# A two-layer hybrid encoder on eight cores: feature-major activations, layer norms by ones-matmuls, two tiles half a layer apart, packed weights

## The chip, the cores and the metric

The kernel runs on all eight cores of one Trainium2 chip (two dies of four cores). The metric is the device time of one execution on the slowest core, in microseconds (us). The times of this kernel come in two states. In the fast state all eight cores show the same granted TensorE clock; in the slow state one die or both show a lower one and the run is some per cent longer.

Names in the text and the profiles: PE is TensorE (matmuls), DVE VectorE, ACT ScalarE, POOL GpSimd, SP SyncE, which here only issues transfers. HBM is the chip's memory, SBUF a core's own, PSUM where TensorE puts its results. A transfer lands when its last data have arrived; its landing time counts from its issue.

## The reference

Each core takes one stream of 8192 rows of 1024 features (16 tiles of 512 rows) and one sample tile of 256 rows. Each of two layers does this:

```python
proj = x @ w_in                                   # 1024 -> 2048
u, v, xb, gb, gc, h = split(proj)                 # 512, 512, 256, 256, 256, 256
out_a = u * spatial_gate(layer_norm(v))           # 128-row chunks, 8 heads
out_b = pool_mixer(xb)                            # trailing means 2/4/8/16, minus xb, then 64x64 maps
out_c = gb * conv3(gc * h)
x = layer_norm(ALPHA * x + concat(out_a, out_b, out_c) @ w_out)
x = layer_norm(ALPHA * x + (silu(x @ w_gate) * (x @ w_up)) @ w_down)   # inner width 2816
# ... states of pool and conv, the normalised v of the sample rows
```

Weights and activations arrive as fp32; both kernels multiply in bf16. One tile of 512 rows through one layer is called a *tile-layer* below. A core does 32 of them, plus two of half the size.

## The kernel before

Weights are converted once per run from fp32 to bf16 in HBM, by casting DMAs on POOL's software queue. For every tile-layer they are streamed again, in 47 units of up to 512 KB, into a ring of 15 slots in SBUF, on SP's hardware queue. A ring load waits for the conversion of its unit and for its slot.

```python
def emit_conv(l, ui):                        # on POOL's queue; reads pieces of 1 to 4 KB, writes 512 B to 2 KB
    ...
    if k[0] == "in":
        src = w_in[l, kc0*128:(kc0+nk)*128, c0:c0+512].rearrange("(k p) n -> p k n", p=128)
        jobs.append((dst.rearrange("p (k n) -> p k n", k=nk), src, 0))
    ...

def emit_load(n):                            # on SP's queue
    ti, l, ui = seq[n]
    s_ = n % NSLOT
    S.add("sp", lambda e: e.dma_start(out=ring[:, s_, 0:ne], in_=wbf[l, ui][:, 0:ne]), ...)
```

The residual lies row-major (`xres`, rows on partitions). After each norm it is cast to `xbf` and transposed on TensorE into `xT`, which the next product reads:

```python
def transpose_chunk(c):
    b = alloc1()
    for k in range(8):
        S.add("pe", lambda e, k=k: e.transpose(out=psb(b)[:, k, :], in_=xbf[:, c, k*128:(k+1)*128], identity=idb[:]), ...)
    S.add("act", lambda e: e.copy(out=xT[:, :, c*128:(c+1)*128], in_=psb(b)), ...)
```

The output and down projections (`tm_proj_ln`, matmuls at L765) keep the activations stationary, so that rows come out on partitions; the norm is then 1024 wide, on DVE and ACT:

```python
def stage_a(c):   # DVE: xres = ALPHA*xres + psum, with row sum; ACT: Square with row sum
    S.add("dve", lambda e: e.scalar_tensor_tensor(out=xres[:, c, :], in0=xres[:, c, :], scalar=ALPHA, in1=..., accum_out=lsum[:, c:c+1]), ...)
    ...
def stage_b(c):   # DVE: reciprocal, last pass; ACT: xbf = bf16(xres)
    ...
# one tile after the other, both layers
for ti in range(len(tiles)):
    for l in range(2):
        tile_layer(ti, l, (ti * 2 + l) * NUNIT)
```

Of the kernel before, what the change touches and what calls it, by code (L numbers as in the profile page):

```python
# [12 lines left out]
DFF = 2816  # L13
NFC = 22
ALPHA = float(4 ** 0.25)
EPS = 1e-5
NSLOT = 15
NUNIT = 47
U_V0, U_V1, U_XB, U_GC, U_H, U_U01, U_U23, U_GB, U_OUT0, U_GU0, U_DN0 = 0, 1, 2, 3, 4, 5, 6, 7, 8, 12, 36
N_CORES = 8  # L20
NPT_FULL = 16

# [155 lines left out]

def build(npt, with_sample=True):
    nc = bass.Bass("TRN2", target_bir_lowering=False)  # L180
    NP = npt * 512
# [7 lines left out]
    xp = din("xp", [NP, D])  # L189
    xs = din("xs", [256, D])  # L190
    spool = din("spool", [2, 60, 256])
    sconv = din("sconv", [2, 8, 256])
    ln_mix_g = din("ln_mix_g", [2, D]); ln_mix_b = din("ln_mix_b", [2, D])
    ln_ffn_g = din("ln_ffn_g", [2, D]); ln_ffn_b = din("ln_ffn_b", [2, D])
    v_norm_g = din("v_norm_g", [2, 512]); v_norm_b = din("v_norm_b", [2, 512])
    w_in = din("w_in", [2, D, 2048])
    w_spatial = din("w_spatial", [2, 8, 128, 128])
    b_spatial = din("b_spatial", [2, 8, 128])
    w_pool = din("w_pool", [2, 4, 64, 64])
    pool_scale = din("pool_scale", [2, 256])  # L200
    conv_w = din("conv_w", [2, 3, 256])
    w_out = din("w_out", [2, D, D])
    w_gate = din("w_gate", [2, D, DFF]); w_up = din("w_up", [2, D, DFF])
    w_down = din("w_down", [2, DFF, D])
    ident = din("ident", [128, 128])
    cst = din("cst", [128, 34])

    yp = dout("yp", [NP, D])
    ys = dout("ys", [256, D])
    o_pool_p = dout("o_pool_p", [2, 15, 256])  # L210
    o_pool_s = dout("o_pool_s", [2, 60, 256])
    o_conv_p = dout("o_conv_p", [2, 2, 256])
    o_conv_s = dout("o_conv_s", [2, 8, 256])
    o_v = dout("o_v", [2, 256, 512])

    wbf = nc.dram_tensor("wbf", [2, NUNIT, 128, 2048], BF16).ap()
# [3 lines left out]
    xres = sb("xres", [128, 4, D], F32)  # L220
    xbf = sb("xbf", [128, 4, D], BF16)
    xT = sb("xT", [128, 8, 512], BF16)
    vscr = sb("vscr", [128, 2, 512], F32)
# [6 lines left out]
    cat = sb("cat", [128, 8, 512], BF16)  # L230
    hid = sb("hid", [128, NFC, 512], BF16)
    sscr = sb("sscr", [128, 2, 512], F32)
    lscr = sb("lscr", [128, 2, D], F32)
    mixg = sb("mixg", [128, D], F32); mixb = sb("mixb", [128, D], F32)
    ffng = sb("ffng", [128, D], F32); ffnb = sb("ffnb", [128, D], F32)
    vng = sb("vng", [128, 512], F32); vnb = sb("vnb", [128, 512], F32)
# [3 lines left out]
    ctmp = sb("ctmp", [128, 2, 512], F32)  # L240
    idf = sb("idf", [128, 128], F32)
    idb = sb("idb", [128, 128], BF16)
    cst_sb = sb("cst_sb", [128, 34], F32)
    pscale = sb("pscale", [128, 2, 2], F32)
    cw = sb("cw", [128, 2, 2, 3], F32)
# [3 lines left out]
    stin = sb("stin", [64, 256], F32)  # L249
    stin2 = sb("stin2", [8, 256], F32)  # L250
    sttm = sb("sttm", [128, 1, 256], F32)
    sttm2 = sb("sttm2", [128, 1, 256], F32)
    vst = sb("vst", [128, 4, 6], F32); vmv = sb("vmv", [128, 4, 2], F32); vrs = sb("vrs", [128, 4], F32)
    lsum = sb("lsum", [128, 4], F32); lmean = sb("lmean", [128, 4], F32)
    lnb = sb("lnb", [128, 4], F32); lsq = sb("lsq", [128, 4], F32); lrs = sb("lrs", [128, 4], F32)
# [3 lines left out]
    st = {"pb": 0, "cv": 0, "ld": 0, "io": 0}  # L259
# [6 lines left out]
    def alloc2():  # L266
        if st["pb"] % 2:
            st["pb"] += 1
        b = st["pb"] % 8
        st["pb"] += 2  # L270
        return b

# [3 lines left out]
    def psb(b):  # L276
        return ps[:, b, :].bitcast(BF16).rearrange("p (k n) -> p k n", k=8)

    UL = [("in", 512, 0, 4), ("in", 512, 4, 4)]
    for c0 in (1024, 1536, 1792, 0, 256, 1280):  # L280
        UL.append(("inF", c0))
    for j in range(4):
        UL.append(("out", j))
    for g in range(6):
        for j in range(4):
            UL.append(("gu", g, j))
    for j in range(11):
        UL.append(("down", j))
    assert len(UL) == NUNIT

    def unit_keys(l, ui):
        if UL[ui][0] == "gu":
            return [("wbf", l, ui, 0), ("wbf", l, ui, 1)]
        return [("wbf", l, ui, 0)]

    def emit_conv(l, ui):
        k = UL[ui]
        dst = wbf[l, ui]
        jobs = []
        if k[0] == "in":  # L300
            _, c0, kc0, nk = k
            src = w_in[l, kc0 * 128:(kc0 + nk) * 128, c0:c0 + 512].rearrange("(k p) n -> p k n", p=128)
            jobs.append((dst.rearrange("p (k n) -> p k n", k=nk), src, 0))
        elif k[0] == "inF":
            c0 = k[1]
            src = w_in[l, :, c0:c0 + 256].rearrange("(k p) n -> p k n", p=128)
            jobs.append((dst.rearrange("p (k n) -> p k n", k=8), src, 0))
        elif k[0] == "out":
            j = k[1]
            src = w_out[l, j * 256:(j + 1) * 256, :].rearrange("(k p) n -> p k n", p=128)  # L310
            jobs.append((dst.rearrange("p (k n) -> p k n", k=2), src, 0))
        elif k[0] == "gu":
            _, g, j = k
            nf = 4 if g < 5 else 2
            f0 = 4 * g
            for wi, wsrc in enumerate((w_gate, w_up)):
                src = wsrc[l, j * 256:(j + 1) * 256, f0 * 128:(f0 + nf) * 128].rearrange("(k p) n -> p k n", p=128)
                d = dst[:, wi * 2 * nf * 128:(wi + 1) * 2 * nf * 128].rearrange("p (k n) -> p k n", k=2)
                jobs.append((d, src, wi))
        else:  # L320
            j = k[1]
            src = w_down[l, j * 256:(j + 1) * 256, :].rearrange("(k p) n -> p k n", p=128)
            jobs.append((dst.rearrange("p (k n) -> p k n", k=2), src, 0))
        for d, s_, wi in jobs:
            ch = st["cv"] % 8
            st["cv"] += 1
            S.add("pool", lambda e, d=d, s_=s_: e.dma_start(out=d, in_=s_),
                  writes=[("wbf", l, ui, wi), ("cvch", ch)], dma_chan=("cv", ch))

    tiles = [("p", t) for t in range(npt)] + ([("s", 0)] if with_sample else [])  # L330
    seq = [(ti, l, ui) for ti in range(len(tiles)) for l in range(2) for ui in range(NUNIT)]

    def emit_load(n):
        ti, l, ui = seq[n]
        s_ = n % NSLOT
        ne = 1024 if (UL[ui][0] == "gu" and UL[ui][1] == 5) else 2048
        S.add("sp", lambda e: e.dma_start(out=ring[:, s_, 0:ne], in_=wbf[l, ui][:, 0:ne]),
              reads=unit_keys(l, ui), writes=[("ring", s_)], dma_chan=("w", s_))

    def slot(n):  # L340
        assert n < st["ld"], (n, st["ld"])
        return n % NSLOT

    def done(n):
        m = n + NSLOT
        assert m == st["ld"], (m, st["ld"])
        if m < len(seq):
            emit_load(m)
        st["ld"] += 1

    def tile_src(ti):
        kind, t = tiles[ti]
        if kind == "p":
            return xp[t * 512:(t + 1) * 512, :], yp[t * 512:(t + 1) * 512, :], 4
        return xs, ys, 2

    def load_xres(ti):
        src, _, nch = tile_src(ti)
        for c in range(nch):
            S.add("pool", lambda e, c=c: e.dma_start(out=xres[:, c, :], in_=src[c * 128:(c + 1) * 128, :]),  # L360
                  writes=[("xres", c)], dma_chan=("xl", c))

    def load_xbf(ti):
        src, _, nch = tile_src(ti)
        for c in range(nch):
            S.add("pool", lambda e, c=c: e.dma_start(out=xbf[:, c, :], in_=src[c * 128:(c + 1) * 128, :]),
                  writes=[("xbf", c)], dma_chan=("xb", c))

    load_xbf(0)
    load_xres(0)  # L370
    for l in range(2):
        for ui in range(NUNIT):
            emit_conv(l, ui)
    for n in range(5):
        emit_load(n)

    def pdma(fn, reads=(), writes=()):
        ch = st["io"]
        st["io"] += 1
        return S.add("sp", fn, reads=list(reads), writes=list(writes), dma_chan=("pr", ch))  # L380

    pdma(lambda e: e.dma_start(out=idf[:], in_=ident), writes=["idf"])
    pdma(lambda e: e.dma_start(out=cst_sb[:], in_=cst), writes=["cst"])
    S.add("act", lambda e: e.copy(out=idb[:], in_=idf[:]), reads=["idf"], writes=["idb"])
    S.add("dve", lambda e: e.memset(epst[:], EPS), writes=["eps"])
# [20 lines left out]
    for var, src_bf, keys in ((0, catA, [("cat", j) for j in range(4)]), (1, catB, [("cat", j) for j in range(4, 8)])):  # L406
        for l in range(2):
# [7 lines left out]
            if var == 0:  # L415
                S.add("dve", lambda e, s0=s0: e.memset(wsT[64:128, s0:s0 + 8, 0:64], 0.0), writes=[("wsT", s0)])
# [495 lines left out]
```

## Time and profile before

| | before |
|---|---|
| three first runs | 6115.57, 6364.31, 6601.76 us (median 6364.31) |
| fast runs (all batches) | 6107 to 6139 us |
| one tile-layer in mid-run, clock 0.99 to 1.00 | 170.2 us |

The page of the profile of the kernel before: first each engine's busy time, its share of the span and its number of instructions; then the span in 40 slices of about 157 us, in tenths (PE busy, PE's granted clock, DMA engines busy); then the shares of the chain of waits that ended last.

```profile
PE 5665.5 (90%) x29197; PEld 2825.2 (45%) x29684; DVE 2400.3 (38%) x4131; ACT 1674.3 (27%) x2801; POOL 532.4 (8%) x622
...
PE   0865799999999999999999999999999999999987
...
PEclk9977899999999999999999999999999888888877
DMA  9999645454455545454544445554555434443354
...
PE 73%; DVE 11%; DMA 10%; ACT 2%; issue 2%; POOL 1%; another core or an unknown queue 1%; DVEq 0%; POOLq 0%; SPq 0%; ACTq 0%
```

TensorE is the bound from within the fifth slice on. Before that the DMA engines are full and PE is not. This profiled execution was one of the slower ones: the clock falls in the last quarter. A tile-layer at 0.81 takes 200.1 us instead of 170.2.

The timeline of PE in mid-run, kernel before. The columns are: start, duration, engine, line, operation, out<-in, shape, count, and in brackets the idle time just before and what ended it. The last line starts the same stage one tile-layer later, and so gives the 170.2 us.

```profile
3129.49 0.39 PE L707 MATMUL ps<-diff,wpbd 128*128 128x512 bf16 x1 [0.40 <-DVE cat L699]
...
3133.63 13.98 PE L765 MATMUL ps<-ring,cat 128*128 128x512 bf16 x62
3147.44 1.06 PE L464 MATMUL ps<-idb,xbf 128*128 128x128 bf16 x16
3150.16 7.15 PE L814 MATMUL ps<-xT,ring 128*128 128x256 bf16 x64 [1.66 <-ACT xT L466]
3158.09 1.15 PE L464 MATMUL ps<-idb,xbf 128*128 128x128 bf16 x16 [0.78 <-ACT sscr L817]
3161.18 69.32 PE L814 MATMUL ps<-xT,ring 128*128 128x256 bf16 x346 [1.94 <-ACT xT L466]
...
3303.83 13.98 PE L765 MATMUL ps<-ring,cat 128*128 128x512 bf16 x63
```

Each pair of transposed chunks (L464) costs 1.1 us of PE and then 1.7 to 1.9 us of waiting for ACT to copy the result out of PSUM.

The waits of PE from 710 us to the end, kernel before (engine, tile and line, releaser: total us, times, longest):

```profile
PE ps L814 <- ACT xT L466: 107.9, 62, 1.9
...
PE ps L707 <- DVE sscr L694: 36.0, 29, 6.6
```

The start costs as much as two tile-layers: PE runs without gaps from 713 us on, and until then it has done two tile-layers, 340 us of work. So 373 us are lost there.

### The profile page before, as it was taken

The numbers are of one execution on the slowest core, as the hardware profiler recorded it, in microseconds if no ns is written. First come the engines' busy times: TensorE is split into PE (matmuls) and PEld (weight loads), VectorE is DVE, ScalarE is ACT, GpSimd is POOL, SyncE is SP. The second block draws the span as 40 slices with busy tenths as digits, with TensorE's granted clock in tenths as the row PEclk, the third lists the DMA queues.
The fourth block names the chain that finished last, engine by engine and source line by source line (L and its number), as shares of the span: only waits on it lengthen the run. The fifth ranks groups of instructions, "written<-read, shape, count | busy, mean of one in ns | idle before, by whom it ended". The sixth has DMA issues, their size and how long they took to land.

```text
span 6285.8 us, 71667 instructions; the slowest of 8 cores (6193.5 to 6285.8 us)
## 1 busy us (share of the span) xinstructions
PE 5665.5 (90%) x29197; PEld 2825.2 (45%) x29684; DVE 2400.3 (38%) x4131; ACT 1674.3 (27%) x2801; POOL 532.4 (8%) x622
## 2 busy tenths in 40 slices
PE   0865799999999999999999999999999999999987
PEld 0422344444444444444444444444444444444454
DVE  0331344333344444444333444444444323442322
ACT  0221232222223232322232322323232222222212
POOL 2111000000000000000000000000000000000000
PEclk9977899999999999999999999999999888888877
DMA  9999645454455545454544445554555434443354
GB/s 134 183 162 161 197 160 184 156 172 163 145 188 174 171 158 185 165 181 165 181 161 160 168 152 190 166 176 161 183 166 181 144 116 170 135 169 128 120 192 155
DMA packets 347184, 1033.95 MB, mean 164 GB/s; under 512 B 42036, under 2 KB 82406, under 8 KB 346854
## 3 DMA queue, kind: packets, MB, share of 16 engines
q1 hardware_dynamic: 268550, 894.39, 42.0%
q0 software_dynamic: 78304, 134.94, 11.4%
q8 instruction: 234, 3.83, 0.3%
q14 instruction: 96, 0.79, 0.0%
HBM read 1057.85 MB, written 83.01 MB: 181 GB/s over the span
## 4 chain that ended last, share of the span: by engine, by line
PE 73%; DVE 11%; DMA 10%; ACT 2%; issue 2%; POOL 1%; another core or an unknown queue 1%; DVEq 0%; POOLq 0%; SPq 0%; ACTq 0%
PE ps L814 37%; PE ps L765 24%; PE ps L575 8%; DMA wbf<-w_gate 3%; DMA wbf<-w_up 3%; PE ps L515 3%; DVE xres L749 2%; DVE xres L727 2%; DVE lscr L740 2%; DMA wbf<-w_in 1%; DVE diff L660 1%; ACT xT L466 1%; PE ps L464 1%; DMA wbf<-w_down 1%; DMA xbf<-xp 1%
## 5 line engine op out<-in xcount | busy, mean ns | idle before, releaser
L814 PE MATMUL ps<-xT,ring 128*128 128x512 bf16 (+1 forms) x13824 | 2667.8, 357 | 188.0 <-ACT xT L466 114.4
L814 PEld LDWEIGHTS ps<-xT,ring 128*128 128x128 bf16 x14016 | 1419.2, 102 | 1422.2 <-issue 308.9
L765 PE MATMUL ps<-ring,hid 128*128 128x512 bf16 x5676 | 1323.6, 393 | 57.2 <-DMA ring<-wbf 49.1
L819 DVE TENSOR_TENSOR hid<-sscr,ps 128x512 bf16<-128x512 f32 (+1 forms) x876 | 517.2, 596 | 2211.6 <-PE ps L814 2116.0
L817 ACT ACTIVATE sscr<-ps 128x512 f32<-128x512 f32 (+1 forms) x876 | 454.2, 524 | 2063.8 <-PE ps L814 2054.3
L765 PEld LDWEIGHTS ps<-ring,hid 128*128 128x128 bf16 x5808 | 581.0, 101 | 777.4 <-issue 196.4
L575 PE MATMUL ps<-xT,ring 128*128 128x512 bf16 (+1 forms) x3182 | 746.9, 387 | 16.0 <-DVE sscr L694 8.6
L727 DVE SCALAR_TENSOR_TENSOR xres<-xres,ps 128x1024 f32<-128x1024 f32 x264 | 321.9, 1219 | 1095.7 <-PE ps L765 1095.7
L731 ACT ACTIVATE xbf<-xres 128x1024 bf16<-128x1024 f32 x264 | 279.0, 1057 | 1387.3 <-DVE xres L727 1387.1
L575 PEld LDWEIGHTS ps<-xT,ring 128*128 128x128 bf16 x3264 | 315.4, 101 | 382.2 <-issue 91.9
L765 PE MATMUL ps<-ring,cat 128*128 128x512 bf16 x2064 | 476.5, 390 | 3.5 <-DMA ring<-wbf 0.6
L765 PEld LDWEIGHTS ps<-ring,cat 128*128 128x128 bf16 x2112 | 210.8, 100 | 263.6 <-issue 58.6
L515 PE MATMUL ps<-ring,xT 128*128 128x512 bf16 x1023 | 247.2, 394 | 65.3 <-ACT xT L466 63.3
L466 ACT COPY xT<-ps 128x1024 bf16<-128x1024 bf16 x264 | 254.7, 1017 | 142.8 <-PE ps L464 142.8
L645 POOL TENSOR_TENSOR pscr<-xbuf 128x526 f32<-128x526 f32 (+1 forms) x64 | 71.3, 1113 | 2345.9 <-ACT xbuf L582 2172.9
L753 ACT CAST xbf<-xres 128x1024 bf16<-128x1024 f32 x198 | 206.9, 1045 | 226.5 <-DVE xres L749 226.5
L464 PE MATMUL ps<-idb,xbf 128*128 128x128 bf16 x2112 | 151.1, 226 | 85.5 <-DMA xbf<-xp 51.6
L755 POOL DMA_DIRECT2D yp<-xres x64 | 34.2, 535 | 1893.4 <-DVE xres L749 1873.5
L515 PEld LDWEIGHTS ps<-ring,xT 128*128 128x128 bf16 x1056 | 104.8, 101 | 195.7 <-issue 76.7
L464 PEld LDWEIGHTS ps<-idb,xbf 128*128 128x128 bf16 x2112 | 133.1, 101 | 125.4 <-DMA xbf<-xp 52.8
L678 POOL TENSOR_TENSOR ybuf<-ybuf,ctmp 128x512 f32<-128x512 f32 (+1 forms) x128 | 180.5, 1420 | 5.0
L749 DVE SCALAR_TENSOR_TENSOR xres<-lscr,lrs,ffnb 128x1024 f32<-128x1024 f32 x132 | 169.6, 1285 | 7.7 <-DVE lrs L748 0.5
(94 smaller groups left out, 2447.5 us busy)
## 6 DMA issues: line engine op xcount, KB each, us to landing
ring<-wbf SPq DMA_DIRECT2D x1462, 512.0 KB, 6.1
ring<-wbf SPq DMA_DIRECT2D x136, 256.0 KB, 4.5
xres<-xp POOLq DMA_DIRECT2D x64, 512.0 KB, 12.7
yp<-xres POOLq DMA_DIRECT2D x64, 512.0 KB, 6.4
mixg<-ln_mix_g SPq DMA_DIRECT2D x34, 512.0 KB, 5.7
mixb<-ln_mix_b SPq DMA_DIRECT2D x34, 512.0 KB, 4.8
ffng<-ln_ffn_g SPq DMA_DIRECT2D x34, 512.0 KB, 11.5
ffnb<-ln_ffn_b SPq DMA_DIRECT2D x34, 512.0 KB, 12.0
```

Source lines behind the costliest of these rows:

```text
L464: S.add("pe", lambda e, k=k: e.transpose(out=psb(b)[:, k, :], in_=xbf[:, c, k * 128:(k + 1) * 128], identity=idb[:]), reads=[("xbf", c), " ...
L466: S.add("act", lambda e: e.copy(out=xT[:, :, c * 128:(c + 1) * 128], in_=psb(b)), reads=[PS(b)], writes=[("xT", c)])
L515: S.add("pe", lambda e, c=c, kc=kc, b=b, w=w: e.matmul(ps[:, b, :], lhsT=xT[:, kc, c * 128:(c + 1) * 128], rhs=w, start=(kc == 0), stop=(k ...
L575: S.add("pe", lambda e, kc=kc, b=b, w=w: e.matmul(ps[:, b, 0:T], lhsT=w[:, kc, j * 128:(j + 1) * 128], rhs=xT[:, kc, 0:T], start=(kc == 0) ...
L727: S.add("dve", lambda e: e.scalar_tensor_tensor(out=xres[:, c, :], in0=xres[:, c, :], scalar=ALPHA, in1=ps[:, pb:pb + 2, :].rearrange("p a ...
L731: S.add("act", lambda e: e.activation(out=xbf[:, c, :], in_=xres[:, c, :], func=AF.Square, accum_out=lsq[:, c:c + 1]), reads=[XK], writes= ...
L749: S.add("dve", lambda e: e.scalar_tensor_tensor(out=xres[:, c, :], in0=lscr[:, c % 2, :], scalar=lrs[:, c:c + 1], in1=bet[:], op0=ALU.mult ...
L753: S.add("act", lambda e: e.copy(out=xbf[:, c, :], in_=xres[:, c, :]), reads=[XK], writes=[("xbf", c)])
L765: S.add("pe", lambda e, k=k, hf=hf, w=w: e.matmul(ps[:, pb + hf, :], lhsT=src[:, k, c * 128:(c + 1) * 128], rhs=w[:, hf * 512:(hf + 1) * 5 ...
L814: S.add("pe", lambda e, kc=kc, b=b, w=w: e.matmul(ps[:, b, t0:t1], lhsT=w[:, kc % 2, fi * 128:(fi + 1) * 128], rhs=xT[:, kc, t0:t1], start ...
L817: S.add("act", lambda e: e.activation(out=sscr[:, f % 2, t0:t1], in_=ps[:, banks[0], t0:t1], func=AF.Silu), reads=[PS(banks[0])], writes=[ ...
L819: S.add("dve", lambda e: e.tensor_tensor(out=hid[:, f, t0:t1], in0=sscr[:, f % 2, t0:t1], in1=ps[:, banks[1], t0:t1], op=ALU.mult), reads= ...
```

## The change

The intent: take the transposes and their copies away by keeping the features on partitions all through; compute the norm's sums over features with matmuls against ones; hide the norm of one tile behind the products of another; and store the weights packed, so that each conversion reads whole 8 KB rows. Cut to its core:

```diff
-UL = [("in", 512, 0, 4), ...]      # 47 units; pieces of 512 B to 2 KB written
+wpk = din("wpk", [2, NUNIT, 128, 2048])          # 45 units, packed on the host
+wbf = nc.dram_tensor("wbf", [2, NUNIT, 128, WROW], BF16).ap()      # WROW = 2304
+    S.add("pool", lambda e: e.dma_start(out=wbf[l, ui, :, 0:2048], in_=wpk[l, ui]), ...)
-NSLOT = 15
+NSLOT = 10
-def transpose_chunk(c): ...                       # 64 PE transposes and 8 ACT copies per tile-layer
-def tm_proj_ln(...): ...                          # row-major products and 1024-wide norms
+def acc(tl, which, l, d, b):                      # feature block d of 8; beside the product
+    S.add("dve", ... xr = xr*ALPHA*g + psum ...)                   # L487
+    S.add("act", ... Square(xr + bias) ...)                        # L490
+    S.add("dve", ... S1 += xr + bias ...)                          # L495
+    S.add("dve", ... S2 += square ...)                             # L497
+def ln_task(tl, which, l):                        # in small steps, in the background
+    # S1, S2 split into bf16 high and low (L510, L511), four ones-matmuls (L519),
+    # mean, variance, Sqrt, 512-wide reciprocal (L530), then per block:
+    S.add("dve", ... xr = xr + bias - mu ...)                      # L538
+    S.add("dve", ... xr = xr * rsd ...)                            # L540
+    S.add("act", ... xt = xr*g + b, bf16 ...)                      # L547
-for ti in range(len(tiles)):
-    for l in range(2): tile_layer(ti, l, ...)
+# stage_order: in/out of tile A, second half of gate/up and down of tile B,
+# first half of gate/up of A, in/out of B, second half and down of A, first half of B, ...
+for o in order:
+    for pe_us, dve_us in stage(o):
+        bg.advance(max(0.1 * pe_us, 0.9 * pe_us - dve_us))         # norm steps by credit
 # head pairs of the spatial gate
+        if j == 1:                                 # the pooling matmuls: after pair 1, were after pair 3
+            ... ps = wpbd * diff ...                               # L743
```

Two more moves: the order converts layer 0 first and needs layer 1 only after two and a half tiles, where before the first tile needed both, one after the other. And the sample tile runs early, among the prompt tiles, where before it ran last. Besides, the host now hands over the inputs with features first and turns the outputs back (`make_in_maps`, `gather`), so the transposes of the first layer's input are gone from the chip altogether; host time is not in the metric.

## The prediction

> **What bounds it now.** TensorE: in the stretch table it is busy 153 of every 160 us from 800 us on; the chain of waits is 73% PE, 11% DVE, 10% DMA. One tile-layer (512 rows, one layer) in mid-run takes 170.2 us on the PE timeline at granted clock 0.99. Its 730 matmuls of 512 columns run at 216 ns (gate/up: 69.2 us for 320), so 157.7 us is the product itself. The other 12.5 us: 64 transposes (4.2 us) and waits for the transposed copy and the pooling result (about 8 us).
>
> Two other costs. Start: until 670 us the DMA engines are full (0.97 to 1.05) while weights are converted to bf16; at 710 us one tile (340 us of work) is done, so about 370 us are lost. Clock: on core 2 it is 0.81 from 4900 us on, on core 0 until 1600 us; a tile-layer then takes 200.1 us. The Trainium skill, "TensorE: Matmul & The Clock Gate", Part 1, names such a 13/16 limit; the 0.81 agrees, though all cores also run long at 0.99. Unthrottled, before would take about 6060 us; the spread 6115 to 6602 is, I think, time at 0.81.
>
> **Removed.** Transposes and their ACT copies (1.02 us each), casts, 1024-wide layer norms, reloaded gains: 12.5 us of PE per tile-layer, less what is added.
> **Added.** Eight ones-matmuls (1.7 us). DVE: per feature block and norm three 512-wide passes while accumulating and two while normalising, 0.69 to 0.76 us each by like forms in the trace; a 512-wide reciprocal, estimated at 3.5 us from 157 ns at 1 and 178 ns at 4 elements. Estimated sum 100 us of DVE per tile-layer against 72 before, ACT about 60: still under 160. In the output projection DVE needs 2.1 us per block against PE's 1.73; eight PSUM banks absorb that.
> **Moved.** Norms run while PE works on the other tile, so their latency leaves the chain. The pooling matmul moves two head pairs earlier while DVE gets two conv passes more (1.5 us a block): there I expect a new PE wait of 2 to 5 us per tile-layer. Weight units are consumed one per 3.45 us; landing takes 6 us, so ten slots suffice.
> **Start.** Conversions read 8 KB rows instead of 1 to 4 KB pieces, and the first two and a half tiles need layer 0 alone. PE dense from 100 to 150 us, saving 250 to 300 us.
>
> **Sum.** Unthrottled: 120 + 32 x 164 + 2 x 85 (sample tile) + 20 = about 5560 us; wholly at 0.81, with 198 us per tile-layer, about 6660. I allow a third of the run at 0.81: 5850 us, range 5480 to 6300. Faster by over 2%: 0.88; within 2%: 0.07; slower: 0.05.
>
> **Right if** a mid-run tile-layer at clock 0.99 takes 161 to 166 us, PE idle in it is under 6 us and mostly before the pooling and output projection matmuls; DVE 60 to 67% busy; DMA no longer full before 500 us, PE over 90% from 200 us on. **Wrong if** PE waits for DVE in gate/up or the output projection, ring loads wait in mid-run, or conversions still starve PE at 400 us.
>
> **What would make it wrong.** Mostly the clock: if steadier matmuls keep all cores at 0.81, the time nears 6600 and the gain is gone. Next, the DVE sum: some passes beside POOL take 1.6 us against 0.76; if that spreads to the new ones, DVE becomes the bound.

## More of the kernel before

The DMA queues of the kernel before from 0 to 640 us (queue and kind: packets, MB, share of the time of 16 engines). q0 is POOL's queue with the conversions, q1 is SP's with the ring loads:

```profile
q0 software_dynamic: 49160, 48.70, 66.6%
q1 hardware_dynamic: 23873, 53.78, 33.3%
```

## The result, and the profile after

| | before | after |
|---|---|---|
| runs of the first batch | 6601.76, 6364.31, 6115.57, 6107.39 us | 5773.33, 5772.45, 5773.61 us; one slow run 6361.02 us |
| median of the batch | 6239.94 us | 5773.47 us |
| ratio of fast runs | | 0.9449 (95%: 0.9427 to 0.9470) |
| tile-layer in mid-run, full clock | 170.2 us | 161.3 us |
| PE without gaps from | 713 us | 614 us |

A ratio is the mean time of one kernel's fast runs over that of the other's in the same rounds, so it is not quite the ratio of the medians. The kernel after is 5.5% faster. In its slow run one die had the clock at 0.872 to 0.876 and the other at 0.974 to 0.976.

The page after, in the same order as before:

```profile
PE 5359.3 (93%) x25852; PEld 2460.9 (43%) x25852; DVE 3285.3 (57%) x4768; ACT 1967.9 (34%) x3021; POOL 206.9 (4%) x282
...
PE   3546989899999999999999999999999999999998
...
PEclk9768999999999999999999999999999999999999
DMA  9999655574445544555445544555445544655443
...
PE 83%; DVE 9%; another core or an unknown queue 4%; DMA 2%; ACT 1%; SPq 1%; issue 0%; DVEq 0%
```

PE is now 83% of the chain. DVE rose from 38% to 57% of the span, and in mid-run PE waits for it only 1.5 us per tile-layer (below). But the first four digits of the DMA line have not changed: the start is as full as before.

The timeline of PE in mid-run, kernel after, from the in-projection of tile A to that of tile B, which is 161.3 us later:

```profile
3093.31 7.07 PE L596 MATMUL ps<-ring,xtA 128*128 128x512 bf16 x32
...
3119.61 0.39 PE L743 MATMUL ps<-diff,wpbd 128*128 128x512 bf16 x1 [0.85 <-DVE diff L680]
...
3126.62 12.48 PE L768 MATMUL ps<-cat,ring 128*128 128x512 bf16 x57 [0.15 <-DVE cat L736]
3138.94 10.52 PE L788 MATMUL ps<-xtB,ring 128*128 128x512 bf16 x48
3149.30 1.03 PE L519 MATMUL ps<-shl,ones 128*128 128x512 bf16 x4
3150.16 20.88 PE L788 MATMUL ps<-xtB,ring 128*128 128x512 bf16 x96
...
3254.62 7.07 PE L596 MATMUL ps<-ring,xtB 128*128 128x512 bf16 x32
```

After the output projection of A (L768), PE goes straight on with gate/up of tile B (L788), and the ones-matmuls of A's norm (L519) slip in without a gap.

The waits of PE from 1300 to 5700 us, kernel after:

```profile
PE ps L743 <- DVE diff L680: 23.0, 27, 0.9
PE ps L638 <- DVE cat L715: 7.4, 27, 0.3
PE ps L726 <- DVE cat L715: 5.5, 27, 0.2
PE ps L768 <- DVE cat L736: 4.2, 25, 0.5
```

These are 1.5 us per tile-layer, all near the pooling matmul; nothing waits for a transposed copy or a ring load.

The stretch table of one tile-layer, first kernel before, then after. The columns are the stretch, its length, the busy time of PE, PE weight load, DVE, ACT and POOL (with numbers of instructions), PE's clock, DMA share, GB/s.

```profile
3133.60:3303.80 170.20, 161.85 (x867) 80.95 (x882) 71.89 (x125) 52.06 (x85) 10.36 (x8) 1.00 0.46 159
```

```profile
3093.30:3254.60 161.30, 159.81 (x763) 71.99 (x762) 98.05 (x138) 59.19 (x90) 6.39 (x8) 1.00 0.58 180
```

So the 8.9 us of a tile-layer are 2.0 us less PE work (transposes out, ones-matmuls in) and 6.9 us less idle (8.35 before, 1.49 after).

The DMA queues of the kernel after from 0 to 640 us:

```profile
q0 software_dynamic: 17632, 50.67, 64.0%
q1 hardware_dynamic: 18467, 54.19, 34.3%
```

The conversions went from 49160 packets to 17632, and they take about the same time: 0.666 x 640 us x 16 engines / 48.7 MB is 140 us of one engine per MB before, and 129 after. The start lost its 373 us before (713 - 340). After, by 614 us, PE had done the in- and output projections of two tiles and the sample tile, all of gate/up and down of tile 0 and four blocks of the next: an estimate of 240 us, from the counts of those matmuls at 216 ns for 512 columns. So some 374 us are lost, as many as before. (Before, PE then has no gap over 2 us up to 1250 us; after, from 614 to 1250 us, it still idles 42 us in all, for norms, the sample tile and the pooling matmuls, with 2 us of waiting for a ring load.)

The whole difference between fast runs, 6113 (profile of the second run of before, below) minus 5772, is 341 us: 32 x 8.9 = 285 in the tile-layers, nothing at the start, and so some 56 elsewhere, at the sample tile and the end. (Before, the sample tile ran last, from 5841 to 6098 us, with 22 us of waiting for its state; after, it is inside the stream and the tail is 28 us.) This last part is accounted for, not isolated by a run.

### The profile page after: what moved, and what is told of

Same layout as the page of the kernel before. It is cut to its first block, busy times and chain, and to the rows that moved or that the text cites. A ratio compares the mean times of both kernels' runs of the same rounds, so it can differ in the third digit from the quotient of the medians.

```text
span 5771.8 us, 63969 instructions; the slowest of 8 cores (5762.9 to 5771.8 us)
## 1 busy us (share of the span) xinstructions
PE 5359.3 (93%) x25852; PEld 2460.9 (43%) x25852; DVE 3285.3 (57%) x4768; ACT 1967.9 (34%) x3021; POOL 206.9 (4%) x282
## 4 chain that ended last, share of the span: by engine, by line
PE 83%; DVE 9%; another core or an unknown queue 4%; DMA 2%; ACT 1%; SPq 1%; issue 0%; DVEq 0%
PE ps L788 43%; PE ps L808 22%; PE ps L768 7%; PE ps L638 6%; PE ps L596 4%; DVE ybuf L697 2%; DMA ring<-wbf 1%; DVE diff L680 1%; DVE cat L736 1%; PE ps L519 1%; ACT ybuf L694 1%; DVE zscr L731 1%; DVE zbuf L690 1%; DVE cat L715 1%
## 5 line engine op out<-in xcount | busy, mean ns | idle before, releaser
L788 PE MATMUL ps<-xtA,ring 128*128 128x512 bf16 x5632 | 1247.4, 383 | 48.2 <-DMA ring<-wbf 47.3
L808 PE MATMUL ps<-hid,ring 128*128 128x512 bf16 (+1 forms) x5984 | 1270.5, 375 | 21.9 <-DMA ring<-wbf 21.9
L788 PE MATMUL ps<-xtB,ring 128*128 128x512 bf16 x5632 | 1229.8, 380 | 8.6 <-DMA ring<-wbf 8.6
L808 PEld LDWEIGHTS ps<-hid,ring 128*128 128x128 bf16 x5984 | 586.9, 98 | 700.1 <-DMA ring<-wbf 26.8
L788 PEld LDWEIGHTS ps<-xtA,ring 128*128 128x128 bf16 x5632 | 554.1, 99 | 730.3 <-DMA ring<-wbf 56.8
L788 PEld LDWEIGHTS ps<-xtB,ring 128*128 128x128 bf16 x5632 | 551.8, 98 | 676.9 <-DMA ring<-wbf 9.3
L768 PE MATMUL ps<-cat,ring 128*128 128x512 bf16 (+1 forms) x2176 | 474.8, 377 | 62.6 <-DMA ring<-wbf 56.9
L638 PE MATMUL ps<-xtB,ring 128*128 128x512 bf16 x1536 | 348.4, 382 | 11.6 <-DMA ring<-wbf 7.7
L638 PE MATMUL ps<-xtA,ring 128*128 128x512 bf16 x1536 | 348.4, 382 | 4.0 <-DVE cat L715 3.9
L768 PEld LDWEIGHTS ps<-cat,ring 128*128 128x128 bf16 x2176 | 212.3, 99 | 320.9 <-DMA ring<-wbf 60.3
L497 DVE TENSOR_TENSOR S<-S,sq 128x512 f32<-128x512 f32 (+1 forms) x476 | 322.1, 677 | 6.2 <-ACT sq L490 3.3
L638 PEld LDWEIGHTS ps<-xtB,ring 128*128 128x128 bf16 x1536 | 145.7, 98 | 187.4 <-issue 9.7
L530 DVE RECIPROCAL rsd<-rsd 128x512 f32<-128x512 f32 (+1 forms) x68 | 221.1, 3251 | 3.5 <-ACT rsd L527 3.5
L638 PEld LDWEIGHTS ps<-xtA,ring 128*128 128x128 bf16 x1536 | 145.9, 98 | 179.1 <-issue 10.2
```

The costliest lines, as they stand in the source:

```text
L497: S.add("dve", lambda e: e.tensor_tensor(out=S2[:, 0:T], in0=S2[:, 0:T], in1=o2, op=ALU.add), reads=["S2", k2], writes=["S2"])
L530: S.add("dve", lambda e: e.reciprocal(out=rsd[:, 0:T], in_=rsd[:, 0:T]), reads=["rsd"], writes=["rsd"])
L638: S.add("pe", lambda e, kc=kc, b=b, w=w: e.matmul(ps[:, b, 0:T], lhsT=w[:, kc * 256 + j * 128:kc * 256 + (j + 1) * 128], rhs=tl.xt[:, kc, ...
L768: S.add("pe", lambda e, d=d, k=k, i=i, b=b, w=w: e.matmul(ps[:, b, 0:T], lhsT=w[:, (d % 2) * 1024 + k * 128:(d % 2) * 1024 + (k + 1) * 128 ...
L788: S.add("pe", lambda e, kc=kc, b=b, w=w, wi=wi: e.matmul(ps[:, b, 0:T], lhsT=w[:, wi * 1024 + kc * 128:wi * 1024 + (kc + 1) * 128], rhs=tl ...
L808: S.add("pe", lambda e, k=k, b=b, w=w, q=q: e.matmul(ps[:, b, 0:T], lhsT=w[:, (q % 16) * 128:(q % 16 + 1) * 128], rhs=hid[:, k, 0:T], star ...
```

## The experiments

Three questions: why did the start gain nothing; which part of the change made the tile-layer shorter; and is there anything left. Two theories of the start stood at first. Theory A: the layer-1 conversions, which nothing needs yet, take the DMA engines from the ring loads; the size of their pieces doesn't matter. The rival: the size of the pieces sets the speed of the conversions, and bigger ones at least helped. From the third run on a third theory took over, called R below: each DMA engine serves one packet of each backlogged queue in turn, so that the queue with the longer packets gets the larger share of the engine's time.

### The kernel before, again

No edit. The first profile of before fell in a slower execution, so it was taken once more.

> The kernel before once more, for a profile in the fast state (the first one fell in a slower execution with a clock of 0.93 to 0.94). Both theories: 6100 to 6120 us if fast. If the start costs what the first profile showed, tensor work reaches the second tile at about 710 us, and a mid-run tile-layer takes 170.2 us; then the fast-state gain of about 335 us is 32 x 8.9 = 285 us of steady state and only some 50 us of start.

Measured: 6114.47 us fast (6531.9 slow); the profiled execution was fast, cores 6091.5 to 6112.9 us, clock 0.965 to 0.967 on all. Mid-run tile-layer 170.2 us and PE without gaps from 713 us, as in the first profile. So the readings above hold for the fast state. The stretch from 0 to 713 us, this run of before, and that from 0 to 614 us, after:

```profile
0.00:713.00 713.00, 370.05 (x1798) 176.23 (x1829) 150.20 (x269) 112.41 (x176) 106.39 (x161) 0.83 0.96 159
```

```profile
0.00:614.00 614.00, 310.03 (x1262) 127.99 (x1262) 191.03 (x331) 96.93 (x166) 58.17 (x114) 0.81 1.00 161
```

Both move 160 GB/s with the DMA engines full. (The clock shown here is low on both, but it is not the slow state. In these two profiles every core is granted either 1.00 or 0.50, never 0.81, and here the 0.50 comes where PE stands still: from 127.2 to 168.2 us of the kernel after PE is busy for 5.8 us, and the clock is 0.50.)

What SP's queue, which issues the ring loads, waits for in the start tells the two kernels apart. Kernel before, second run, 100 to 700 us:

```profile
SPq L162 <- DMA wbf<-w_up: 175.6, 30, 13.3
SPq L337 <- DMA wbf<-w_down: 127.3, 22, 8.5
SPq L337 <- DMA wbf<-w_in: 51.6, 7, 11.7
```

Kernel after, 100 to 600 us:

```profile
SPq L168 <- PE ps L788: 121.7, 22, 8.4
SPq L353 <- PE ps L808: 59.5, 10, 8.6
...
SPq L353 <- DMA wbf<-wpk: 16.2, 9, 6.7
```

Before, the ring loads wait for the conversions, and once issued they land in 10 to 14 us from 300 us on. After, they hardly wait for conversions in this stretch (16 us in all): they are issued as soon as PE frees a slot, and then take 55 to 61 us to land. The idle time is as long and has another cause: the bound has moved from the conversions' order to the sharing of the DMA engines. Not all of it is ring loads: PE's own waits for these are 111 of 341 us before (up to 713 us) and 169 of 304 after (up to 640). The largest others are the set-up before the first product (124 us before, 66 after), tile 1's input before (57) and the sample tile after (34.5).

### Layer 0 converted only

The layer-1 conversions are left out and both layers use layer 0's weights. Its output is wrong, which doesn't matter for the time.

```diff
-    convs = [(l, ui) for l in range(2) for ui in range(NUNIT)]
+    convs = [(0, ui) for ui in range(NUNIT)]
-    ... in_=wbf[l, ui, :, 0:2048], reads=[("wbf", l, ui)]
+    ... in_=wbf[0, ui, :, 0:2048], reads=[("wbf", 0, ui)]
```

> The changed kernel with the conversion of layer 1's weights left out; layer 1 uses layer 0's weights, so the outputs are wrong on purpose. Theory A (the start is bound by the bytes that the DMA engines must move: about 4.4 us per converted unit and about 2 us per ring load, whatever the piece size): the DMA engines are full only until about 330 us, TensorE is dense from about 340 us instead of 614 us, the whole takes 5500 to 5580 us. Theory B (the start is bound by something else, such as the order of units or the issue of single loads): DMA is still full or TensorE still starved at 450 us, and the time falls by less than 100 us.

Measured: 5656.96 us, fast. The DMA engines are full only until about 320 us, and from about 356 us PE doesn't wait for weights any more (one gap of 13 us, at 380 us, is a norm's). That is 116 us less than the kernel after, and not the 190 or more that theory A needed for 5500 to 5580: layer 0's own conversions starve the ring as well (before 356 us PE waits 101 us for ring loads).

### Smaller pieces: 1 KB written per row and piece

```diff
-    wpk = din("wpk", [2, NUNIT, 128, 2048])
+    wpk = din("wpk", [2, NUNIT, 4, 128, 512])       # same bytes, in four blocks; packed so by the host
-    e.dma_start(out=wbf[l, ui, :, 0:2048], in_=wpk[l, ui])
+    e.dma_start(out=wbf[l, ui, :, 0:2048].rearrange("p (k n) -> p k n", k=4), in_=wpk[l, ui].rearrange("k p n -> p k n"))
```

> The changed kernel with the packed weights laid out in four blocks per unit, so that each conversion reads 2 KB pieces and writes 1 KB pieces, as most of the kernel before's did. Theory A (bytes): the packets of the software queue rise about threefold, the time that the queue's packets take and the end of the full-DMA phase (about 600 us) stay within 5%, total 5770 to 5800 us. Theory of my prediction (piece size sets the conversion rate): the full phase lasts 100 us or more longer, total 5870 us or more.

Measured: correct, 5633.07 us fast (two slow runs 6537.4 and 6547.44). This is 140 us *faster* than the kernel after; one theory said the same, the other slower. Both fell. The last conversion is issued at 780 us, where it was 575: the conversions are slower, and the kernel is faster. The DMA queues from 450 to 500 us, where both have work waiting:

```profile
q1 hardware_dynamic: 2401, 8.75, 59.5%
q0 software_dynamic: 2424, 2.41, 43.4%
```

The two queues have equal numbers of packets, 2401 and 2424. For the kernel after, from 400 to 600 us:

```profile
q0 software_dynamic: 4481, 16.32, 64.9%
q1 hardware_dynamic: 4512, 16.44, 35.3%
```

Again equal numbers. In the second, a conversion packet takes 0.649 x 200 us x 16 / 4481 = 463 ns (3.6 KB); in the first, 0.434 x 50 x 16 / 2424 = 143 ns (1.0 KB). (Sizes and times of packets are means over a queue, here and below. They include the 4 bytes that end a transfer on each engine, in the kernel after one packet in nine beside eight of 4 KB.) Ring packets take 200 to 250 ns in both. The share follows from the packet's time. The Trainium skill, "DMA: Bandwidth & Descriptors", section "Queues, rings and completion order", says that each engine goes round the queues that have work, and changes only at packet boundaries; the equal counts agree. That is theory R. PE's busy time in the 100 us from 100 us on rises from 42 to 63 us, from 400 us on from 65 to 92, and its waits for ring loads in the whole start fall from 169 to 82 us.

### Layer-1 conversions paced

Each layer-1 conversion is issued only when a certain ring load has landed, spread over ring loads 60 to 177; layer 0's are as they were.

```diff
+    at = min(PACE0 + i*(PACE1 - PACE0)//(NUNIT - 1), first[(1, i)] - 14)    # PACE0 = 60
+    paced.setdefault(at, []).append((1, i))
 # in emit_load(n): this load also writes ("ld", n), and then
+    for cl, cu in paced.pop(n, ()): emit_conv(cl, cu, n)                     # reads ("ld", n)
-    convs = [(l, ui) for l in range(2) for ui in range(NUNIT)]
+    convs = [(0, ui) for ui in range(NUNIT)]
```

> The changed kernel with layer 1's conversions spread out: each waits until a given ring load has landed, from load 60 to load 177, instead of all being queued at once. Same bytes, same results. Theory A (the start is bound by DMA bytes, and layer 1's conversions take the bandwidth that the first ring loads need): TensorE waits for ring loads fall from about 200 us to about 100 us, dense from about 350 us, total 5560 to 5640 us. Theory B (the conversion's total time has to pass whatever the order): total within 50 us of 5773 us.

Measured: correct, 5679.03 to 5680.78 us in four fast runs (6630.82 slow); against before 0.9266 (0.9241 to 0.9291). This is 94 us less than the kernel after, less than expected. PE is 100% busy from 400 to 600 us, but still only 32 to 60% before 400: pacing frees the ring from layer 1's conversions, not from layer 0's.

### The two-tile order undone

Everything else of the change stays; one tile-layer follows the other. (With the order also goes the late need for layer 1 and the early place of the sample tile.)

```diff
-    ... interleaved items of tiles A and B ...
+    for x in [(t, l) for t in range(npt) for l in range(2)] + [("S", 0), ("S", 1)]:
+        out += [("in",) + x, ("out",) + x, ("gu",) + x + (0, gs), ("gu",) + x + (gs, NFC), ("dn",) + x]
```

> The changed kernel with its two-tile order undone: each tile runs a whole layer before the next stage of another tile starts, everything else the same. Theory A (the removal of transposes needs the second tile, because a feature-major norm cannot start before the last block of a projection, and its chain is some 18 us: two splits, ones-matmuls, three copies, a 3.25 us reciprocal, eight normalised blocks at 1.44 us): TensorE waits about 15 to 20 us at each of about 51 exposed norms, a tile-layer takes about 190 us at full clock, the whole 6500 to 6800 us, slower than before. Rival (the interleave adds little, since the projections before and after hide the norm): under 5900 us.

Measured: correct, 7412.51, 7571.02 and 7643.86 us; worse than expected, and no run was fast (in the profile die 0 had clock 0.836 and 7360 to 7411 us, die 1 0.887 and 7067 to 7083 us). But core 4 of die 1 was not disturbed: its trace has no 0.81, of which core 0 has 2383 us, only 1.00 and 0.50. Its 7067 us can be compared: 1295 us more than the kernel after. The timeline of PE from the end of an output projection, core 4, where matmuls run at 216 ns:

```profile
2148.11 12.48 PE L768 MATMUL ps<-cat,ring 128*128 128x512 bf16 x57 [0.15 <-DVE cat L736]
...
2175.46 0.58 PE L788 MATMUL ps<-xtA,ring 128*128 128x512 bf16 x1 [7.91 <-ACT xtA L547]
...
2185.10 76.91 PE L788 MATMUL ps<-xtA,ring 128*128 128x512 bf16 x345 [0.78 <-ACT xtA L547]
```

From 2160.6 to 2185.1 us, 24.5 us, PE waits for the norm, with only the ones-matmuls and single first matmuls in between. Of a tile's four norms three are waited for: two gaps of 22 to 24.5 us, and one of 37 us, together about 84 us per tile in the stretch read. With 16 prompt tiles an estimate is 5772 + 16 x 84 = 7116 us, near core 4's 7067. So feature-major norms alone would have made the kernel much slower: they are longer in latency than those they replace, and the interleave is what hides them. The part and its hiding place are one change, not two.

### The kernel before without transposes

Each chunk of `xT` is transposed once, in the first tile, and then reused. Its output is wrong, which doesn't matter for the time. Everything else of before stays.

```diff
+    tr = set()
     def transpose_chunk(c):
+        if c in tr:
+            return
+        tr.add(c)
```

> The kernel before with every transpose after the first tile's first layer left out, so that the matmuls reuse old transposed data; outputs wrong on purpose. It bounds what the transposes and the waits for their results cost. Theory A (they are nearly all of the steady gain): a mid-run tile-layer takes 159 to 161 us against 170.2, the whole 5760 to 5810 us, about the changed kernel's time. Rival (the gain comes from the interleave, the even weight units or the packed rows): a tile-layer stays above 165 us.

Measured: 6065.86, 6110.84, 6564.46 us, all slow. In the profile the four cores of die 1 have no 0.81 in their traces and took 5920 to 5929 us, where those of the fast profile of before took 6092 to 6113: some 180 of the 341 us of the whole change. The timeline of PE on core 4:

```profile
2074.02 71.94 PE L819 MATMUL ps<-xT,ring 128*128 128x256 bf16 x352 [3.50 <-ACT sscr L822]
...
2183.79 7.07 PE L520 MATMUL ps<-ring,xT 128*128 128x512 bf16 x32
...
2348.76 7.07 PE L520 MATMUL ps<-ring,xT 128*128 128x512 bf16 x32
```

A tile-layer takes 165.0 us here and 166.1 the one before, 165.5 in the mean, not the 159 to 161 expected. The transposes and their waits give 4.7 of the 8.9 us, and the number lies at the edge of the rival, which named the interleave or the weights. In their place a wait of 3.5 us appears at gate/up: the silu (L822) stands behind the norm's work on ACT, which goes on until 2072.3 us there. This wait is most of the 4.2 us that are still missing to 161.3; the rest of the gain needed the norm out of the way, which is what the interleave does. The weights have nothing to give there: in mid-run PE waits for no ring load in either kernel.

### The row pitch of the converted weights

```diff
-WROW = 2304
+WROW = 2048
```

The destination rows become contiguous. This was to test whether the padding had made ring loads land sooner in mid-run (6.1 us before, 3.7 after).

> The changed kernel with rows of the bf16 weights in memory 4096 bytes apart instead of 4608. Theory A (landing of a ring load fell from 6.1 to 3.7 us because the loads are spaced evenly): landing stays 3.5 to 4 us, total within 20 us of 5773 us. Rival (the padded pitch spreads the rows over the memory better): landing above 5 us, the DMA share in mid-run higher than 0.48, total perhaps unchanged in mid-run but the start longer by 50 us or more.

Measured: correct, 5895.0 us fast (6803.04 slow), 122 us slower than the kernel after. Mid-run is unchanged (landing 3.3 us, the same waits): the padding is not what shortened the landing. The loss is at the start, which the rival allowed for (50 us or more), but for a reason that neither theory had named. The DMA queues from 200 to 500 us:

```profile
q0 software_dynamic: 1859, 30.45, 90.0%
q1 hardware_dynamic: 1861, 5.79, 9.6%
```

The counts are equal once more, but a conversion packet now holds 30.45 MB / 1859 = 16.4 KB and takes 0.9 x 300 x 16 / 1859 = 2.3 us in the mean. In the trace half of them are the 4 bytes that end a transfer; each of the others holds 32 KB, the eight rows of 4 KB that one engine has of a unit run together, and takes 4.6 us. The ring gets a tenth of the engines. The longest wait of PE for a ring load is 202.3 us. The padding, whatever it was put in for, keeps packets at one row.

### The pooling matmul one pair later, with small pieces

The kernel with small pieces, and the pooling matmuls after head pair 2, to take away the 0.85 us wait at L743.

```diff
-            if j == 1:
+            if j == 2:
```

> The changed kernel with 2 KB conversion pieces (as in the run with pieces) and the pooling matmuls one head pair later. Expected from the pieces: 5630 us. From the later pooling matmuls: their wait of 0.85 us and most of the 0.5 us that follow go in every tile-layer, 161.3 to about 160.1 us, so 5580 to 5600 us. Rival for the second part (the wait moves to the output projection, since DVE is behind by the same amount): a tile-layer stays at 161 us, total 5630 us.

Measured: correct, 5649.19, 5631.13 and 5630.86 us fast (three slow); against before 0.9215 (0.9175 to 0.9254). The tile-layer is still 161.3 us: the wait at the pooling matmul is gone, and 0.95 us of idle stands before the output projection instead (with 0.27 and 0.38 us between). So the wait is DVE's time in this stretch and not the place of the matmul; this edit is worth nothing, and the time is that of the smaller pieces alone.

### Two and eight pieces

As in the third run, with `k=2` (2 KB written per piece) and `k=8` (512 B). These two were to test theory R.

> The changed kernel with the packed weights in two blocks per unit: conversions read 4 KB and write 2 KB pieces. Theory R (the engines serve one packet of each queue in turn, so a queue's share is set by its packet's time): where both queues are backlogged the packet counts of the two queues are equal, the software queue's share lies between the 43% of the 1 KB pieces and the 65% of the 4 KB ones, about 55%, and ring loads get about 6.3 MB per 50 us against 4.1 with 4 KB pieces. Total between 5630 and 5700 us. Rival (pieces of any size below 4 KB help alike because the issue of conversions on POOL becomes slower): shares as with 1 KB pieces, 5630 us, and packet counts not equal.

Measured: 5689.29, 5694.37 and 5699.3 us fast (two slow). The DMA queues from 350 to 400 us:

```profile
q0 software_dynamic: 1738, 3.35, 55.7%
q1 hardware_dynamic: 1740, 6.34, 46.8%
```

Equal counts, a share of 55.7% and 6.3 MB for the ring in 50 us, as theory R had said (about 55%, 6.3 MB).

> The changed kernel with eight blocks per unit: conversions read 1 KB and write 512 B pieces. Theory R: equal packet counts where both queues are backlogged, the software queue's share there about 35%, and ring loads take what they ask; conversions end later than 780 us, and TensorE waits for units that are not converted yet instead of for ring loads behind conversions. Total 5620 to 5750 us, so no large gain over 1 KB pieces. Against theory R: a share above 50% with both backlogged.

Measured: correct, 5636.7 us fast (6609.75 slow), within the range expected. Only in short stretches are at least seven of the ten ring loads in flight (issued and not landed). The DMA queues in one of them, 650 to 675 us:

```profile
q1 hardware_dynamic: 1588, 5.79, 68.4%
q0 software_dynamic: 1713, 0.86, 35.2%
```

The counts are nearly equal and the share is 35%, as theory R had said (from 425 to 450 us, with six or more in flight, it is 1722 packets to 1532, and 35.8%). With fewer ring loads in flight the conversions get more than every second turn: from 450 to 500 us, with four to seven, 4582 packets to 2107, and 52%. If these few loads left some of the engines without a ring packet, that agrees with theory R; the traces don't tell the engines apart, so it is not shown. SP's queue now waits 126 us for units that aren't converted yet (100 to 800 us; 140 with 1 KB pieces, 16 in the kernel after). Below 1 KB nothing more was won.

### Large pieces for layer 0, small ones for layer 1

Would faster conversions help where layer 0 is awaited?

```diff
+    src, nb = (wpk0, 2) if l == 0 else (wpk1, 4)
+    e.dma_start(out=wbf[l, ui, :, 0:2048].rearrange("p (k n) -> p k n", k=nb), in_=src[ui].rearrange("k p n -> p k n"))
```

> The changed kernel with 4 KB to 2 KB pieces for layer 0's conversions, which TensorE needs soon, and 2 KB to 1 KB pieces for layer 1's, which can wait. Theory R: the wait of about 30 us for units not yet converted near 345 to 430 us (seen with 1 KB pieces) shrinks, the waits for ring loads before it grow a little; total 5600 to 5650 us, near the best that the start allows by packet size alone.

Measured: correct, one fast run of 5631.02 us (five slow). One run, so only this: no gain over four pieces for both layers is seen.

### The series

| conversion packet | fast runs, us | engine time of one packet | share of conversions, both queues waiting |
|---|---|---|---|
| 16.4 KB (no padding) | 5895 | 2.3 us | 90% |
| 3.6 KB (the kernel after) | 5772 to 5774 | 463 ns | 65% |
| 1.9 KB (two pieces) | 5689 to 5699 | 256 ns | 56% |
| 1.0 KB (four pieces) | 5633 | 143 ns | 43% |
| 0.5 KB (eight pieces) | 5637 | 82 to 91 ns | 35% |

The time per KB of a packet (its time over its size) is 127 to 144 ns from 1.0 to 16.4 KB, so larger packets bought no speed; 0.5 KB costs some 160 to 180 ns per KB. Each step down to 1 KB gave the ring a larger share and the kernel a shorter start. (The batches ran on different chips, and the fast runs of before lie between 6107 and 6139 us in them, so differences under some 30 us between batches are not read.)

## Why the prediction was right or wrong

The class and the range were right: 5773 us against 5850 predicted, in a range of 5480 to 6300. The point came out near by errors that cancelled.

**Right: what bounds the kernel, and the tile-layer.** Predicted 164 us, and 161 to 166 as the sign of being right; measured 161.3. Transposes and their waits left the chain; DVE was to be 60 to 67% busy and is 61% (98.05 of 161.3 us). The new DVE passes take 692 to 752 ns (0.69 to 0.76 predicted), the reciprocal 3345 ns (3.5). The wait at the pooling matmul is where it was foreseen, but 1.5 us with its neighbours, not 2 to 5. The term was mis-sized, and 32 tile-layers are 86 us shorter than the sum had them.

**Wrong: the step "Start".** Here the mechanism failed, and not only a number. "Conversions read 8 KB rows instead of 1 to 4 KB pieces" and "PE dense from 100 to 150 us, saving 250 to 300 us". Measured: PE dense from 614 us, saving nothing (374 us lost against 373). The first half failed because conversions cost 129 to 145 us of one engine per MB at any mean packet size from 1.0 to 16.4 KB: bigger rows have hardly any speed to give. The second half, that only layer 0 is needed at first, was true (from 100 to 600 us ring loads wait 16 us for conversions), but its gain was taken back by the first: larger packets gave the conversions 65% of the engines while both queues were full, and the ring loads took 55 to 61 us to land. Cutting the same bytes into 1 KB pieces gives 140 us back, and this was run. The prediction named the sign itself, "conversions still starve PE at 400 us", and it came true; "DMA no longer full before 500 us" and "PE over 90% from 200 us on" did not. What it left out was to ask how two full queues share an engine.

**Wrong: the term for the clock.** "I allow a third of the run at 0.81", some 290 us. Fast runs have none of it: in the profile after, the clock is 1.00 on all eight cores from 1250 to 5740 us, at 99% PE busy. The slow run of after was 6361 us. The unthrottled sum of 5560 us was 213 us below the measured 5773: the start +254 (374 lost against 120 allowed), the tile-layers -86 (161.3 against 164), the sample tile and the end about +45. The allowance for the clock, +290, then hid it. That an allowance for a clock that then stayed at 1.00 covered a start that wasn't foreseen is luck. Put at equal clock, a gain of 8% was predicted (6060 to 5560) and 5.5% came.

**Left open.** Why a run falls into the slow state wasn't studied. The 56 us gained outside tile-layers and start were only accounted for. The experiment with the order undone has no fast run, only undisturbed cores. The ring was also cut from 15 slots to 10, and no run puts them back: from 400 to 600 us eight to ten of the ten loads were in flight and the engines were full, so more slots would by theory R have made a longer queue and not a faster one, but that is argued. The set-up before the first product (66 us) and the sample tile's wait were not tried either.

## What to carry to other kernels

When two DMA queues are both full, count packets: here they were served one for one (4481 to 4512, 2424 to 2401, 1738 to 1740), so the background stream was better cut into packets that take less time than those of the stream that an engine waits for (143 ns against some 200; equal size was not enough, 463 against 250). "Bigger pieces" is a gain only if the time per byte falls with size, which has to be measured. A norm with a longer latency can still be the right one if another tile's products cover it, but then the order is part of the change and has to be costed with it. And check a forecast's terms one by one: a total that comes out right can hold two errors that cancel.

## What the Trainium skill lacked or had wrong

- "DMA: Bandwidth & Descriptors", section "Queues, rings and completion order", states the turn-taking by packet, but not what follows from it: a queue's share is its packet's time over the sum. Runs: conversions at 90, 65, 56 and 43% of the engines with mean packets of 16.4, 3.6, 1.9 and 1.0 KB, and totals of 5895, 5773, 5694 and 5633 us. Beside a queue that TensorE waits for, larger packets cost time in these runs, and the engine time per KB was the same from 1.0 to 16.4 KB (127 to 144 ns).
- The same page, section "SWDGE vs HWDGE vs iDMA", gives a packet as preferably up to 4096 B. With contiguous destination rows the casting DMAs' data packets were 32 KB in the trace (16.4 KB in the mean over all packets); no page says that padding of a row keeps them at one row.
- "TensorE: Matmul & The Clock Gate", Part 1, says that a die goes to 13/16 of the clock soon after three of its cores run dense matmuls, and stays there while the load lasts. These traces neither confirm nor refute the condition. In the fast profile after, all eight cores had PE 99% busy at clock 1.00 from 1250 to 5740 us of their own time; 0.81 was seen in other executions (before: a tile-layer of 200.1 us in place of 170.2). But the traces of two cores share no time, so three cores of a die need not have been busy at one moment: in the slow profile of before, 0.81 lies before 1700 us on cores 0 and 1 and after 4900 us on cores 2 and 3 of the same die.
- The same page, Part 4, gives about 390 ns for one 128x128 transpose alone and about 275 in a kernel, and no rate for transposes back to back. Here one took 226 ns in the mean, and as they overlap, 16 of them took 1.06 us, 66 ns each; what they cost most was the 1.7 to 1.9 us wait for the copy out of PSUM.
